# One inference step of a two-layer hybrid backbone: the last head's rows written into the preparation's buffers, six rows prepared in the loop instead of four, attention's bounds and scales computed in the loop, the key weights issued behind a transpose

## The chip, the core and the metric

The kernel runs on one core of one Trainium2 chip. The metric is the device time of one execution in microseconds (us). A core has five engines with a program of their own each: TensorE for matmuls (PE in the profile, PEld its weight loads), VectorE (DVE), ScalarE (ACT), GpSimd (POOL) and SyncE (SP), which here only issues DMA transfers. They meet through semaphores.

## The reference

Two layers, each a modulated RMS norm, a mixer with a SiLU gate, an output projection and a residual. Layer 0 is bidirectional gated linear attention with 4 heads, layer 1 softmax attention with 8 query and 2 key heads on 1024 latent and 256 cached tokens. The 256 prompt tokens run through both layers too. Width is 1024. Cut to what matters:

```python
def step(S, inp):                       # one chunk of the scan, per head and direction
    qi, ki, vi, gi = inp
    b = jnp.cumsum(gi, axis=2)
    ...
    o = jnp.einsum("bhts,bhsv->bhtv", a, vi) + jnp.einsum("bhtk,bhkv->bhtv", qe, S)
    S = jnp.exp(b_last[:, :, 0, :])[..., None] * S + jnp.einsum("bhsk,bhsv->bhkv", ki * jnp.exp(b_last - b), vi)
...
o = rms_norm(o_f + flip(o_b), onorm).reshape(B, T, GLA_VD)
y = (o * jax.nn.silu(gate)) @ w_out     # gla_mixer
xs = xs + gt_s * out_s                  # the residual
...
q = rms_norm(q.reshape(B, T, ATT_HEADS, HEAD_DIM), qn)    # attn_project
k = rms_norm(k.reshape(B, T, ATT_KV_HEADS, HEAD_DIM), kn)
keys = jnp.concatenate([ks_, cache_k[:, i]], axis=1)
vals = jnp.concatenate([vs, cache_v[:, i]], axis=1)
s = jnp.einsum("bqhgd,bkhd->bhgqk", qblk, keys) * scale
```

## The kernel before

The 1280 tokens are 10 rows of 128 (`NT`); rows 0 and 1 are the prompt. Every large product is made of three matmuls with 16-bit halves (high × high, high × low, low × high), so each activation row and each weight is scaled by a power of two and split into two halves `hi` and `lo`; the inverse of a weight's scale is kept in a column `inv`.

**The loop** (`gla`) has 50 slots, one for each head and row, in ten for each of four heads and ten more in which the last head is only finished. In a slot, the values and gates of a row are made (`value_gate`), one direction's scan is advanced (`outer`, `local`) and the other direction of the head before is finished: `combine` (a scan step: POOL makes the state `Sc` from DVE's `Wc`, PE multiplies it, the output tile is called `o`, `U`, `z` or `cs`, DVE adds and makes the next `Wc`) and `gated` (DVE multiplies with the gate's tile `gx`, SP stores the 256 columns of this head into the DRAM tensor `og_d`). Beside that, `filler` and a list of jobs work on what later parts need: the weights of the next head, the split of the attention's weights into DRAM (`split_ahead`), the output weights (`fill_out`, slots 30 to 38), and in the last slots the first output rows. Weights and other pieces are staged through the pool `wst`, which has two buffers of 1 MB; in the last slots one of them holds the residual's gates (`gate_load`).

**A row of layer 0's output** is prepared by `out_load` (a reload of the row, 128x1024, from `og_d`) and `out_prep` (absolute maximum on DVE, a power of two, the high half on ACT, the low half on DVE, two DMA transposes on SP into `hT_hi` and `hT_lo`), and used by `residual` (72 matmuls on PE into the banks `y`, 24 of them 128x512 and 48 of them 128x256, in the loop into the banks `A` and `kt`; scale and add on DVE) and by the modulation for layer 1. Four rows (2 to 5) are prepared in the loop, and two of them (2 and 3) get their residual there.

**`gla_out`** makes the other rows after the loop: per row n the residual, the preparation of row n + 2, the modulation (`mod_tile`, with two transposes) and the keys and values of an earlier row (`key_tile`, 48 matmuls into the bank `kv`, transposes into `kT`). At its start it loads the cache and the key weights `w_kv` (four transfers on SP) and computes what attention needs: `att_setup` the bounds, that is the largest absolute values of the norms' weights and of the cached keys and values, taken over the partitions by matmuls against the identity (`pow2`), and `key_setup` the scales of keys and values.

The order on each engine is set when the program is built: a scheduler simulates the program, and each piece has a priority that the table `LATER` shifts by name. An engine runs its instructions, and SP its transfers, in that fixed order. `issue_after(x)` puts a piece behind the instruction x in the order.

Of the kernel before, what the change touches and what calls it, by code (L numbers as in the profile page):

```python
# [17 lines left out]
P = 128  # L18
D = 1024
# [20 lines left out]
PREP = (42, 43, 45, 46)  # L40
EARLY = (45, 47)
# [31 lines left out]
    "x.prep": -90,  # L73
# [3 lines left out]
    "x.mod": 60,  # L77
# [18 lines left out]
    "gate9": 220,  # L96
    "combine9": -140,
    "jobs9": -150,
    "filler9": 150,
    "x.key8": 150,  # L100
    "eres": 100,
    "emod": -40,
# [4 lines left out]
    "x.key": -30,  # L107
# [17 lines left out]
LN_EXP_SET = 6  # L125


class K:
# [151 lines left out]
    def split_ahead(self, name, j, st):  # L280
# [7 lines left out]
        keep[j] = self.t(self.const, [P, 1], F32, f"inv_{name}{j}")  # L288
# [547 lines left out]
    def gated(self, h, i, og, r, g):  # L836
        nc = self.nc
        nc.vector.scalar_tensor_tensor(g, og, r, g, ALU.mult, ALU.mult)
        nc.sync.dma_start(self.og_d[i, :, h * DV : h * DV + DV], g)
# [17 lines left out]
    def gla_init(self):  # L857
# [4 lines left out]
        self.jobs = []  # L862

# [148 lines left out]
    def gla_out(self, wo, early, n0):  # L1012
# [3 lines left out]
        self.inv_h = self.inv_h1  # L1016
# [14 lines left out]
        for n in range(n0, NT):  # L1031
# [36 lines left out]
            if n == n0:  # L1068
                d, inv = self.ahead["kv"]
                wkv = []  # L1070
                for j, (hi, lo) in enumerate((
                    [t[:, :, 256:512] for t in self.nw[0:2]], (half[:, 0], half[:, 1])
                )):
                    nc.sync.dma_start(hi, d[:, j, 0])
                    nc.sync.dma_start(lo, d[:, j, 1])
                    wkv.append((hi, lo, 256))
                with self.tc.issue_after(last):
                    with self.later("x.setup"):
                        self.att_setup(*ckv)
                    with self.later("x.kset"):  # L1080
                        self.key_setup(*ckv, inv)
# [80 lines left out]
    def att_load(self):  # L1162
# [6 lines left out]
        c = self.t(self.wst, [P, KT, 256], F32, "wst").rearrange("p k n -> p (k n)")  # L1169
        ck, cv = (c[:, 512 * j : 512 * j + 512].rearrange("p (t h d) -> p t h d", t=2, h=2) for j in range(2))  # L1170
        nc.sync.dma_start(ck, I["cache_k"][0, 0].rearrange("(t p) h d -> p t h d", p=P))
        nc.sync.dma_start(cv, I["cache_v"][0, 0].rearrange("(t p) h d -> p t h d", p=P))
        return ck, cv

    def att_setup(self, ck, cv):
        nc, ap = self.nc, self.ap
        m = self.t(self.sm, [P, 4], F32, "amx", bufs=1)
        for j, t in enumerate((self.qn, self.kn)):
            nc.vector.tensor_reduce(m[:, j : j + 1], t, AX.X, ALU.max, apply_absolute_value=True)
        nc.vector.tensor_scalar(m[:, 0:2], m[:, 0:2], 16.0, None, ALU.mult)  # L1180
        for j, t in enumerate((ck, cv)):
            nc.vector.tensor_reduce(
                m[:, 2 + j : 3 + j], t.rearrange("p t h d -> p t (h d)"), AX.XY, ALU.max, apply_absolute_value=True
            )
        nc.vector.tensor_tensor(m[:, 1:2], m[:, 1:2], m[:, 2:3], ALU.max)
        s, inv = self.pow2(m, 4)
        self.asc = self.t(ap, [P, 4], F32, "asc")
        nc.vector.tensor_copy(self.asc, s)
        self.sexp = self.t(ap, [P, 1], F32, "sexp")
# [659 lines left out]
```

## Time and profile before

| | us |
|---|---|
| median of 3 runs | 1254.11 |
| lowest and highest | 1251.12, 1257.43 |
| the profiled execution | 1256.39 |
| its span, first to last instruction | 1254.6 |
| PE busy | 1193.2 |
| DVE busy | 942.8 |
| ACT busy | 689.5 |

The span is read from left to right: the modulation's weights and first rows until about 95 us, the loop's slots until about 548 us, the output rows of layer 0 with keys and values until about 700 us, attention, and layer 1's output. Line numbers (L214) are those of the kernel before. L214 is the helper that issues all three-fold matmuls, so it is read by its tiles (`mm` values, gates and pieces of queries and keys in the loop, `A` and `kt` the two residuals in the loop, `y` the output rows after it, `kv` the key tiles). In a timeline the value in brackets is the engine's idle time ahead of the instruction, and what ended it.

### The profile page before, as it was taken

To read this page: it belongs to the slowest core of one execution; us is meant where nothing else is said; L and a number is where in the kernel's file an instruction comes from. 1 tells how busy PE (TensorE), PEld (TensorE's weight loads), DVE (VectorE), ACT (ScalarE), POOL (GpSimd) and SP (SyncE) were. 2 spreads that over 40 slices of the span, in tenths; PEclk is the share of its full clock that TensorE was granted. 3 is DMA by queue.
4 is the path that set the end of the run, shared out by engine and by line. 5 is a ranking of instruction groups with operands and counts; after the bars stand their busy time and mean duration, and the time that the engine had idled before them with its cause. 6 is when DMAs were issued, how large, how long until landed. Compare 5 with 4: busy or idle time off the path is not lost. (4 is left out here: it accounts for less than half of the span.)

```text
span 1254.6 us, 22383 instructions
## 1 busy us (share of the span) xinstructions
PE 1193.2 (95%) x7990; PEld 781.4 (62%) x7990; DVE 942.8 (75%) x2188; ACT 689.5 (55%) x1698; POOL 326.6 (26%) x566
## 2 busy tenths in 40 slices
PE   4899999999999999898999899999999999989998
PEld 3467765655556557665776666767766657665444
DVE  4787879879788799769875687877766687785653
ACT  2664666647656567623333577666676676663110
POOL 0132123223321243311213434332232342310000
PEclk9999999999999999899999999999999999999999
DMA  9511565456555545589974887767868466978432
GB/s 377 194 65 73 202 210 191 160 176 207 164 180 179 159 124 164 142 237 248 260 191 130 182 157 132 140 132 151 185 135 151 110 123 132 195 139 208 163 135 84
DMA packets 317664, 209.74 MB, mean 167 GB/s; under 512 B 257094, under 2 KB 294254, under 8 KB 309232
## 3 DMA queue, kind: packets, MB, share of 16 engines
q1 hardware_dynamic: 310400, 190.78, 59.1%
q10 hardware_dynamic: 4688, 10.57, 2.4%
q0 software_dynamic: 2464, 6.95, 1.9%
q8 instruction: 63, 1.03, 0.3%
q14 instruction: 49, 0.40, 0.1%
HBM read 107.57 MB, written 39.35 MB: 117 GB/s over the span
## 5 line engine op out<-in xcount | busy, mean ns | idle before, releaser
L214 PEld LDWEIGHTS <-hT_hi 128*128 128x128 f16 x1920 | 187.8, 98 | 120.6 <-DMA hT_hi<-oghl 3.8
L214 PE MATMUL mm<-whi,hT_hi 128*128 128x512 f16 (+1 forms) x576 | 200.2, 348 | 0.5 <-ACT gx L679 0.4
L214 PE MATMUL mm<-whi,hT_lo 128*128 128x512 f16 (+1 forms) x576 | 200.3, 348 | 0.0
L214 PE MATMUL mm<-wlo,hT_hi 128*128 128x512 f16 (+1 forms) x560 | 194.2, 347 | 0.9 <-DVE wlo L276 0.9
L214 PEld LDWEIGHTS <-whi 128*128 128x128 f16 x1232 | 120.2, 98 | 63.8 <-issue 4.4
L1285 PE MATMUL S<-kT,wst 128*128 128x512 f16 (+1 forms) x624 | 140.2, 338 | 7.1 <-ACT p L1293 6.1
L214 PE MATMUL mm<-hT_hi,whi 128*128 128x256 f16 (+1 forms) x480 | 141.0, 294 | 3.7 <-ACT gx L1328 2.4
L1318 DVE SCALAR_TENSOR_TENSOR phl<-p,srec,phl 128x1280 f16<-128x1280 f32 (+1 forms) x80 | 107.0, 1337 | 49.5 <-ACT phl L1317 33.3
L214 PE MATMUL mm<-hT_lo,whi 128*128 128x256 f16 (+1 forms) x480 | 141.0, 294 | 0.0
L214 PE MATMUL mm<-hT_hi,wlo 128*128 128x256 f16 (+1 forms) x480 | 141.0, 294 | 0.0
L214 PEld LDWEIGHTS <-hT_lo 128*128 128x128 f16 x960 | 94.2, 98 | 62.5 <-issue 1.3
L214 PE MATMUL mm<-PT,vh 128*128 128x256 f16 x672 | 117.9, 279 | 9.3 <-DMA PT<-phl 6.3
L1288 DVE TENSOR_REDUCE smx<-S 128x1 f32<-128x1280 f32 (+1 forms) x80 | 101.3, 1271 | 27.0 <-PE S L1285 26.9
L1293 ACT ACTIVATE p<-S,snb,sexp 128x1280 f32<-128x1280 f32 (+1 forms) x80 | 99.1, 1238 | 12.6 <-DVE phl L1318 7.2
L1285 PEld LDWEIGHTS <-wst 128*128 128x128 f16 x624 | 60.9, 98 | 57.3 <-issue 7.1
L214 PE MATMUL mm<-PT,vl 128*128 128x256 f16 x336 | 93.9, 279 | 0.0
L1315 POOL TENSOR_SCALAR phl<-p,srec 128x1280 f16<-128x1280 f32 (+1 forms) x40 | 52.8, 1319 | 107.0 <-DVE srec L1309 62.7
L214 PEld LDWEIGHTS <-vh 128*128 128x128 f16 x672 | 66.7, 100 | 21.1 <-issue 6.0
L214 PEld LDWEIGHTS <-wlo 128*128 128x128 f16 x616 | 60.2, 98 | 29.8
L1124 POOL TENSOR_TENSOR rope<-hx,ropet 128x64 f32<-128x64 f32 x160 | 53.3, 363 | 84.0 <-ACT hx L1249 61.6
L237 DVE TENSOR_REDUCE wmx<-wst 128x1 f32<-128x512 f32 x104 | 65.1, 675 | 3.0 <-DMA wst<-in_att_w 2.0
L205 POOL TENSOR_TENSOR hrs<-hrsa,mhalf 128x2 f32<-128x2 f32 x50 | 39.5, 792 | 81.2 <-DVE hrsa L203 80.7
(383 smaller groups left out, 2682.7 us busy)
## 6 DMA issues: line engine op xcount, KB each, us to landing
wada<-in_w_ada SPq DMA_DIRECT2D x16, 1024.0 KB, 5.4
wst<-in_att_w SPq DMA_DIRECT2D x14, 1024.0 KB, 5.4
wst<-in_gla_w_in SPq DMA_DIRECT2D x12, 1024.0 KB, 5.3
og_d<-gx SPq DMA_DIRECT2D x40, 128.0 KB, 1.9
og_d<-og POOLq DMA_DIRECT2D x40, 128.0 KB, 3.0
wst<-og_d SPq DMA_DIRECT2D x5, 1024.0 KB, 6.1
xr<-x_d SPq DMA_DIRECT2D x9, 512.0 KB, 3.8
out<-xr ACTq DMA_DIRECT2D x17, 256.0 KB, 2.0
```

What stands on the lines that cost most here:

```text
L205: nc.gpsimd.tensor_tensor(r, a, self.mhalf[:, 0:w], ALU.pow)
L214: self.pe = self.nc.tensor.matmul(out, a, b, start=k == 0 and j == 0, stop=k == n - 1 and j == 2).ins
L237: nc.vector.tensor_reduce(mx[:, j : j + 1], st[:, 2 * j : 2 * j + 2, :], AX.XY, ALU.max, apply_absolute_value=True)
L1124: nc.gpsimd.tensor_tensor(tv[:, h, :, w, :], xv[:, h, :, 1 - w, :], sn[:, :, w, :], ALU.mult)
L1285: nc.tensor.matmul(S[:, a : a + n], x, y, start=m == 0, stop=m == 2)
L1288: last = nc.vector.tensor_reduce(mx, S, AX.X, ALU.max).ins
L1293: nc.scalar.activation(p, S, AF.Exp, scale=self.sexp, bias=nb, accum_out=den)
L1315: nc.gpsimd.tensor_scalar(hi, p, r, 2.0 ** 14, ALU.mult, ALU.mult)
L1318: nc.vector.scalar_tensor_tensor(lo, p, r2, hi, ALU.mult, ALU.subtract)
```

## The change

- Rows 2, 3 and 4 of the last head no longer go through `og_d`. In slot 39 (`ROWS`) their buffers are set up, two rows in one buffer of `wst` and one in a buffer of `split`, and the 768 columns of heads 0 to 2 are loaded into them; `gated` writes the last head's 256 columns there, without a store.
- Six rows (2 to 7) are prepared in the loop, in slots 40, 41, 42, 45, 46 and 48, instead of four in 42, 43, 45 and 46. The two residuals in the loop stand in slots 43 and 46 instead of 45 and 47.
- The bounds are a job of slot 11, with loads of the cache and of the norms' weights of their own (four transfers on SP); the cache is loaded again for its use. The scales are a job of slot 42: five small DVE instructions on a table `inv_a` of all the weights' inverse scales, in place of columns that were multiplied one by one.
- The loads of `w_kv` stand behind the last transpose of the rows prepared in the loop.
- The table `LATER` has other numbers for eight names, and one name less.

The diff, with the parts left out that only rename columns:

```diff
-PREP = (42, 43, 45, 46)
-EARLY = (45, 47)
+ROWS = 39
+PREP = (40, 41, 42, 45, 46, 48)
+EARLY = (43, 46)
...
-    "x.prep": -90,
+    "x.prep": -150,
...
-    "combine9": -140,
-    "jobs9": -150,
-    "filler9": 150,
+    "combine9": 70,
+    "jobs9": 220,
+    "filler9": 15,
...
+BOUNDS, SCALES = 11, 42
...
     def gated(self, h, i, og, r, g):
         nc = self.nc
+        a = slice(h * DV, h * DV + DV)
+        if h == GH - 1 and i in self.direct:
+            nc.vector.scalar_tensor_tensor(self.direct[i][:, a], og, r, g, ALU.mult, ALU.mult)
+            return
         nc.vector.scalar_tensor_tensor(g, og, r, g, ALU.mult, ALU.mult)
-        nc.sync.dma_start(self.og_d[i, :, h * DV : h * DV + DV], g)
+        nc.sync.dma_start(self.og_d[i, :, a], g)
...
-                    nc.sync.dma_start(hi, d[:, j, 0])
-                    nc.sync.dma_start(lo, d[:, j, 1])
+                    with self.tc.issue_after(self.tr):
+                        nc.sync.dma_start(hi, d[:, j, 0])
+                        nc.sync.dma_start(lo, d[:, j, 1])
...
+    def bounds_load(self):
+        t = self.t(self.wst, [P, KT, 256], F32, "wst").rearrange("p k n -> p (k n)")
+        self.cache(t)
+        for j, n in enumerate(("att_qnorm", "att_knorm")):
+            self.nc.sync.dma_start(t[:, D + HD * j : D + HD * j + HD], self.I[n].to_broadcast([P, HD]))
+        return self.bounds, t
+
+    def bounds(self, t):
+        nc = self.nc
+        m = self.t(self.small, [P, 4], F32, "wmx")
+        nc.vector.tensor_reduce(
+            m[:, 2:4], t[:, 0:D].rearrange("p (j n) -> p j n", j=2), AX.X, ALU.max, apply_absolute_value=True
+        )
+        nc.vector.tensor_reduce(
+            m[:, 0:2], t[:, D : D + 2 * HD].rearrange("p (j n) -> p j n", j=2), AX.X, ALU.max,
+            apply_absolute_value=True,
+        )
         nc.vector.tensor_scalar(m[:, 0:2], m[:, 0:2], 16.0, None, ALU.mult)
...
         s, inv = self.pow2(m, 4)
...
+            if slot == BOUNDS:
+                k.jobs.append(k.bounds_load())
+            if slot == SCALES:
+                k.jobs.append((k.scales,))
...
+            if slot == ROWS:
+                t = k.t(k.wst, [P, KT, 256], F32, "wst").rearrange("p k n -> p (k n)")
+                u = k.t(k.spl, [P, 2, KT // 2, 256], F16, "split").rearrange("p j k n -> p (j k n)").bitcast(F32)
+                for n, a in enumerate((t[:, 0:D], t[:, D:], u)):
+                    k.direct[NTP + n] = a
+                for n in (1, 0, 2):
+                    load(k.direct[NTP + n][:, 0 : D - DV], k.og_d[NTP + n, :, 0 : D - DV])
             if slot in PREP:
                 n = PREP.index(slot)
-                a = k.t(k.wst, [P, KT, 256], F32, "wst").rearrange("p k n -> p (k n)")[:, 0:D]
                 b = [k.t(k.qkp, [P, 512], F32, f"{j}{n % 2}").bitcast(F16) for j in "qk"]
-                to = k.out_load(NTP + n, a, b)
+                if NTP + n in k.direct:
+                    to = NTP + n, k.direct[NTP + n], b
+                else:
+                    a = k.t(k.wst, [P, KT, 256], F32, "wst").rearrange("p k n -> p (k n)")[:, 0:D]
+                    to = k.out_load(NTP + n, a, b)
```

Three places of the programs. The first is PE in the last slots of the loop, the steps of the last head's scan (`o`, `U`, `z`, `cs` from `Sc`). Before:

```order
L214 MATMUL mm_6748<-whi_1555_5986,hT_lo_74 128x256
L826 MATMUL o_6680<-Sc_6676,qe_6278 128x256
L826 MATMUL U_6731<-Sc_6727,qe_6141 128x256
L826 MATMUL z_6786<-Sc_6782,qe_6010 128x256
L826 MATMUL cs_6855<-Sc_6851,qe_5893 128x256
L826 MATMUL o_6920<-Sc_6916,qe_5759 128x256
L214 LDWEIGHTS hT_hi_73
```

Five steps stand in a row. After, three stand in a row:

```order
L219 MATMUL mm_6797<-whi_1552_6003,hT_lo_74 128x256
L832 MATMUL o_6703<-Sc_6699,qe_6295 128x256
L832 MATMUL U_6769<-Sc_6765,qe_6158 128x256
L832 MATMUL z_6835<-Sc_6831,qe_6027 128x256
L219 LDWEIGHTS hT_hi_73
```

Then 24 matmuls of a value or gate tile follow, and behind them the next two steps (`cs`, `o`) and 24 more.

The second place is DVE at the same scan, around the fifth `Wc`; `wm` from a row's buffer (`wst` or `split`) is the maximum of a row's preparation. Before:

```order
L795 TENSOR_TENSOR Wc_6918<-Sc_6916,u_1550_5975 128x256
L828 TENSOR_TENSOR og_6922<-o_6920,oa_1554_5984 128x256
L203 TENSOR_SCALAR orsa_6862<-ossq_6860 128x1
L795 TENSOR_TENSOR Wc_7056<-Sc_7054,u_1518_5862 128x256
L203 TENSOR_SCALAR orsa_6927<-ossq_6925 128x1
L783 COPY Wc_7285<-u_1431_5571 128x256
L320 SCALAR_TENSOR_TENSOR ls_6720<-gx_6718,ls_6720 128x256
L1001 TENSOR_REDUCE wm_1783_6799<-wst_6744 128x1
```

After, from the row behind the fourth `Wc`:

```order
L208 TENSOR_SCALAR orsa_6842<-ossq_6840 128x1
L188 TENSOR_SCALAR p2e_6719<-p2c_6717 128x1
L846 SCALAR_TENSOR_TENSOR wst_6581<-og_6705,ors_6712,gx_6622 128x256
L334 TENSOR_TENSOR gx_6756<-gx_6756,ls_6758 128x256
L190 TENSOR_SCALAR p2s_6721<-p2e_6719 128x1
L846 SCALAR_TENSOR_TENSOR split_6582<-og_6771,ors_6778,gx_6690 128x256
L192 TENSOR_SCALAR p2i_6723<-p2e_6719 128x1
L834 TENSOR_TENSOR og_6991<-cs_6989,oa_1593_6136 128x256
L1015 TENSOR_REDUCE wm_1777_6781<-wst_6581 128x1
L801 TENSOR_TENSOR Wc_7054<-Sc_7052,u_1547_5992 128x256
L848 SCALAR_TENSOR_TENSOR gx_6756<-og_6837,ors_6844,gx_6756 128x256
L1015 TENSOR_REDUCE wm_1796_6854<-split_6582 128x1
```

Before, the first row's maximum stands behind the sixth `Wc`. Now the gates are written into the rows' buffers, and the maximum of row 3 stands ahead of the fifth `Wc`, that of row 4 behind it; that of row 2 (not shown) stands ahead of the third.

The third place is SP at the start of the output rows: the loads of the cache, of the key weights `w_kv`, and the transposes of the prepared rows. Before:

```order
L1172 DMA wst_7372<-in_cache_v 128x2x256
L1008 DMA_TRANSPOSE hT_lo_74<-k_1846_7103 128x8x128
L488 DMA_TRANSPOSE hT_hi_73<-split_7019 128x8x128
L488 DMA_TRANSPOSE hT_lo_74<-split_7019 128x8x128
L995 DMA og_7357<-og_d_64 128x1024 x2
L1024 DMA xr_7471<-in_x_sample 128x1024
L1074 DMA whi_1555_5986<-w_kv_1478 128x8x256
L1075 DMA wlo_1556_5987<-w_kv_1478 128x8x256
L839 DMA og_d_64<-gx_7276 128x256
L1074 DMA wkv_7358<-w_kv_1478 128x2048
L1075 DMA wkv_7358<-w_kv_1478 128x2048
```

After:

```order
L1021 DMA_TRANSPOSE hT_hi_73<-q_1882_7349 128x8x128
L849 DMA og_d_64<-gx_7329 128x256
L1187 DMA wst_7423<-in_cache_k 128x2x256
L1188 DMA wst_7423<-in_cache_v 128x2x256
L1022 DMA_TRANSPOSE hT_lo_74<-k_1883_7350 128x8x128
L1088 DMA whi_1552_6003<-w_kv_1481 128x8x256
L1089 DMA wlo_1553_6004<-w_kv_1481 128x8x256
L1009 DMA og_7412<-og_d_64 128x1024
L1037 DMA xr_7508<-in_x_sample 128x1024
L1088 DMA wkv_7413<-w_kv_1481 128x2048
L1089 DMA wkv_7413<-w_kv_1481 128x2048
```

The last gated row's store, which stood between the key weights, now stands ahead of them, and so does the second transpose of row 7 (`k`). The transposes of the early modulation (`split`) stand ahead of the first of these rows.

More of the change, by code (lines that the diff above doesn't have):

```diff
@@ L106 @@
     "wo3": 245,
-    "x.key": -30,
+    "x.key": -150,
     "s.v": 150,
@@ L1347, in load_w @@
         w = self.wload(name, place, later)
[L1348 removed]
+        return w, w[2]
     def query_start(self):
```

81 lines of the change are left out of this document (37 added, 44 removed).

## The prediction, made before the changed kernel ran

> **What bounds the kernel now.** I read the page first: busy time and share of each engine, then the chain of waits that ended last.
>
> ```profile
> PE 1193.2 (95%) x7990; PEld 781.4 (62%) x7990; DVE 942.8 (75%) x2188; ACT 689.5 (55%) x1698; POOL 326.6 (26%) x566
> PE 30%; DMA 4%; DVE 3%; ACT 1%; issue 1%; POOL 0%; ACTq 0%; POOLq 0%; SPq 0%
> ```
>
> TensorE (PE) is busy in 1193.2 of 1254.6 us, so all that waits can give back in the whole program is 61 us. The change takes no matmul away from PE. So the next view is the busy time by windows (window, its length, then busy us of PE, its weight loads, DVE, ACT, POOL; the granted clock; the DMA share) around the places that the change works in: the end of the loop, the first output rows, and what follows.
>
> ```profile
> 498.50:548.10 49.60, 43.97 (x304) 31.74 (x304) 37.76 (x103) 25.45 (x67) 14.28 (x21) 0.93 0.54 146
> 548.10:610.00 61.90, 55.93 (x418) 40.26 (x417) 50.78 (x133) 21.61 (x43) 7.54 (x12) 1.00 1.10 269
> 610.00:700.00 90.00, 90.00 (x667) 65.06 (x665) 62.95 (x141) 32.04 (x89) 27.55 (x60) 1.00 0.76 183
> ```
>
> PE idles 49.60 − 43.97 = 5.6 us in the loop's end, 61.90 − 55.93 = 6.0 us in the first rows, and not at all in the 90 us after: what is won ahead of 610 passes through those 90 us unchanged. In the first row the clock is 0.93, the only dip of the three. The view of PE's waits (engine, line, waited for: us, times, longest) names the causes:
>
> ```profile
> PE y L214 <- DMA hT_hi<-oghl: 3.5, 1, 3.5
> PE kv L172 <- DVE p2e L183: 1.8, 1, 1.8
> PE cs L826 <- POOL Sc L791: 1.6, 1, 1.6
> PE U L826 <- POOL Sc L791: 1.4, 1, 1.4
> PE z L826 <- POOL Sc L791: 0.9, 1, 0.9
> PE y L214 <- DMA hT_lo<-oghl: 0.7, 1, 0.7
> PE o L826 <- POOL Sc L791: 0.6, 1, 0.6
> ```
>
> **Term 1, the output rows.** PE's timeline (start, us, instruction, idle before it and its releaser) places three of them in the output rows:
>
> ```profile
> 548.15 0.38 PE L214 MATMUL y<-whi,hT_hi 128*128 128x512 f16 x1
> ...
> 568.88 0.27 PE L214 MATMUL y<-wada,hT_lo 128*128 128x256 f16 x1
> 570.96 0.23 PE L172 MATMUL kv<-ident,amx 128*128 128x128 bf16 x1 [1.81 <-DVE p2e L183]
> ...
> 579.67 0.39 PE L214 MATMUL y<-whi,hT_hi 128*128 128x512 f16 x1 [3.50 <-DMA hT_hi<-oghl]
> ...
> 593.87 0.39 PE L214 MATMUL y<-whi,hT_lo 128*128 128x512 f16 x1 [0.66 <-DMA hT_lo<-oghl]
> ```
>
> They sum to 5.97, all of the idle time of this window. The first is the bounds' transpose on PE, which stands in PE's order ahead of the first key tile. With the bounds in slot 11 it is not there: −1.81. The other two are rows 6 and 7, whose preparation started only in this phase, and which are now prepared in the loop. When are they ready there? A row needs its store, reload, reduce, two halves and two transposes. Before, four rows do this one behind the other, since one staging buffer is free for the reload:
>
> ```profile
> 523.80 1.22 DVE L1001 TENSOR_REDUCE wm<-wst 128x1 f32<-128x1024 f32 x1 [1.94 <-DMA wst<-og_d]
> ...
> 533.26 1.22 DVE L1001 TENSOR_REDUCE wm<-wst 128x1 f32<-128x1024 f32 x1 [2.04 <-DMA wst<-og_d]
> ...
> 542.45 1.22 DVE L1001 TENSOR_REDUCE wm<-wst 128x1 f32<-128x1024 f32 x1 [2.31 <-DMA wst<-og_d]
> ```
>
> ```profile
> 545.45 1.23 SPq L1007 DMA_TRANSPOSE hT_hi<-q  x1
> ...
> 548.67 1.86 SPq L1008 DMA_TRANSPOSE hT_lo<-k  x1
> ```
>
> A turn is 9.5 us, and the second transpose is issued 6 us behind the reduce (548.67 − 542.45). Rows 2 to 4 now skip store and reload, so only rows 5, 6 and 7 take such turns, in the buffer that rows 2 and 3 leave. The page has the reload (KB, median us to landing):
>
> ```profile
> wst<-og_d SPq DMA_DIRECT2D x5, 1024.0 KB, 6.1
> ```
>
> If the halves of row 3 are out of the buffer near 520 (row 2's came at 518 before, and its reload is gone), row 5's reduce stands near 527, those of rows 6 and 7 near 536 and 546; they are transposed by 542 and 552 and, with an allowance of 7 us for landing, ready by 549 and 559. PE takes 20.8 us for two rows (548.15 to 568.88), so it wants row 6 at about 567 and row 7 behind a key tile at about 583. Some 20 us are in hand: −3.50 − 0.66.
>
> The key weights could be late in their place. Before, they leave SP here:
>
> ```profile
> 557.27 0.38 SPq L1074 DMA_DIRECT2D whi<-w_kv  x1
> ...
> 558.44 4.45 SPq L839 DMA_DIRECT2D og_d<-gx  x1
> 562.92 0.43 SPq L1074 DMA_DIRECT2D wkv<-w_kv  x1
> ```
>
> The second pair stood 4.45 us behind the last gated row's store and was still in time. After, all four stand behind that store and behind row 7's second transpose, so they go at about 553 to 557, and PE reads them from about 568, since the first key tile now stands between the matmuls of row 6. With 6 to 7 us for landing they are there some 4 us ahead. Nothing is added; if row 7 slips by more than that, each further us costs one. Term 1 is **−6.0**; its bounds are −6.0, and −2.5 if the key weights inherit a wait of 3.50.
>
> **Term 2, the scan in the loop's end.** The last head's o steps wait for POOL's Sc, this for DVE's Wc, this for the Sc before:
>
> ```profile
> 503.13 0.70 PE L826 MATMUL U<-Sc,qe 128*128 128x256 f32 x2 [1.36 <-POOL Sc L791]
> 504.68 0.70 PE L826 MATMUL z<-Sc,qe 128*128 128x256 f32 x2 [0.85 <-POOL Sc L791]
> 507.03 1.22 PE L826 MATMUL cs<-Sc,qe 128*128 128x256 f32 x2 [1.65 <-POOL Sc L791]
> 508.88 1.22 PE L826 MATMUL o<-Sc,qe 128*128 128x256 f32 x2 [0.63 <-POOL Sc L791]
> ```
>
> ```profile
> 507.00:509.00 2.00, 1.34 (x3) 0.63 (x3) 1.99 (x7) 0.95 (x4) 1.82 (x3) 0.50 0.19 66
> 509.00:511.00 2.00, 2.00 (x8) 1.32 (x9) 1.10 (x4) 1.15 (x6) 1.50 (x3) 0.50 0.81 195
> 511.00:513.00 2.00, 2.00 (x11) 1.44 (x10) 0.78 (x3) 1.97 (x8) 1.49 (x3) 0.50 0.52 207
> ```
>
> From 507 to 513 PE is busy for 5.3 us at half clock, which is 2.7 us of work: 2.7 more are lost, and no view of waits shows them. The stretch of 49.6 us is thus 5.6 of waits, 2.7 of clock and 41.3 of work. Before, five o steps stand in a row on PE. After, 24 matmuls of 128x256 stand between the third and the fourth (some 2.6 us, at a quarter of the 10.4 us that a row of 24 wide and 48 such matmuls takes) and cover about one step of the chain (1.55, 2.35 and 1.85 us between the starts above). Against that, DVE, which runs the chain and is already full ahead of it, gets the reduces of rows 2, 3 and 4 between its Wc's, each of 1.22:
>
> ```profile
> 475.00:500.00 25.00, 24.07 (x177) 18.83 (x176) 24.51 (x75) 19.83 (x52) 7.47 (x12) 1.00 0.47 148
> ```
>
> I laid DVE's new order over these durations, Wc, Sc, o in turn. Row 2's reduce stands ahead of the third Wc, row 3's ahead of the fifth, row 4's behind it. PE's waits come out as 1.2 in the first three steps, 1.4 and 2.1 at the fourth and fifth, 1.6 for row 2's transposes: 6.3, an estimate. At full clock the stretch takes 41.3 + 6.3 = 47.6, that is −2.0; with the half clock again, 50.3, +0.7; with every wait and the clock won, −8.3. I take **−2.0**, because the low stretch (PE busy 1.34 of 2 us and less) is now broken by dense matmuls.
>
> [...]
>
> **Term 3, the loop at slot 11.** The bounds bring four loads through one staging buffer on SP, ahead of head 2's query and key weights, and on DVE a reduce of 1024 elements (1.22), a short one and some ten small instructions: about 3.5 us. The 16 small instructions that go lay at 564 to 590, where they cost nothing by themselves. Around the place:
>
> ```profile
> 200.00:225.00 25.00, 24.51 (x164) 15.71 (x162) 22.96 (x63) 15.19 (x46) 10.97 (x19) 1.00 0.63 225
> ```
>
> ```profile
> 199.51 0.64 SPq L843 DMA_DIRECT2D wst<-in_gla_w_in  x1
> ...
> 202.95 0.33 SPq L229 DMA_DIRECT2D wst<-in_att_w  x1
> ```
>
> ```profile
> 220.21 0.27 PE L214 MATMUL mm<-hT_hi,whi 128*128 128x256 f16 x1 [0.49 <-ACT gx L679]
> ```
>
> ```profile
> 220.51 2.27 DVE L276 SCALAR_TENSOR_TENSOR wlo<-wst,p2s,whi 128x512 f16<-128x512 f32 x3
> ```
>
> The load of 199.51 takes the turn of 202.95, 3.4 us later, so the fill that ends at 222.78 ends near 226. PE started on that piece at 220.21, beside the fill; about 2 us of other matmuls now go ahead of it. A stall between 0 and 3.4 remains; 3.4 − 2 = 1.4 is left if PE was right behind the fill, less where it was not, and I take **+0.5**. A gain is excluded here: nothing is removed. The remaining edits I cost at nothing: the five scale instructions of slot 42 (0.14 to 0.22 each, counted with the chain's DVE time), the second load of the cache, 0.5 MB on queues that carry 0.54 of their share at 498 to 548, and the table in place of copies.
>
> **Sum.** −6.0 − 2.0 + 0.5 = −7.5. The profiled execution took 1256.39, so its like would take 1248.9; it lies 2.3 above the median of the runs shown, 1254.11, which gives **1246.6**.
>
> **Rivals.** *The scan eats it* (0.25): the three reduces add 1.22 each to PE's waits and the half clock comes again: +3.6 in place of −2.0, so −1.9 in all, 1252. For it: DVE at 24.51 of 25. Against: the 24 matmuls between the steps. *All is won* (0.12): −6.0 − 8.3, 1240. For it: 37.76 of 49.60 us busy on DVE leave room on average; against: the chain's own steps of about 2 us. *The queue falls behind* (0.13), the slower side: SP issues in order, and per output row with its key tile there are six transposes and three loads or stores. PE takes 10.4 + 5.2 = 15.6 us for such a row; transposes at 1.2 to 2.7 us take 7 to 16. The lead of the four rows still prepared in this phase, counted in PE's order, shrinks from about 23 us to 15.6. From the point where SP needs over 15.6 us a row, each of the four waits as row 6 did, 3.50: +14.0, in all +6.5, 1261. For it: the DMA share of 1.10 from 548 to 610. Against: the same load per row at 610 to 700 with PE at 90.00 of 90.00. *The 1.81 is hidden anyway* (within the first): PE would then wait longer for row 6; but 36 and more matmuls stand between the two waits and both are idle time, so they add.
>
> **How the numbers follow.** The forecast has 0.50. A measurement of this kernel can tell some 0.5%, 6.3 us, from no change, so faster means below 1247.8. Three quarters of the forecast (whose own range is 1242 to 1250) lie there, with the large gain: 0.50. Within the bound are its rest and the first rival: 0.35. Slower is the queue's case with the upper end of term 3: 0.15. The range is 1239 (all won) to 1256 (the first rival with 3.4 in term 3).
>
> **What would show it.** Right: no wait of a kv matmul for p2e, none of y for hT from 548 to 610; PE at its whole time from the first y on; the first y near 546; the clock above 0.97 in the loop's end. Wrong: a kv wait for the key weights, a y wait for a transpose, an o wait for Sc above 2.5, a wait for wlo near 220 to 226, or new waits behind 700, where PE's order is the same and the gain should arrive whole.

## The result, and the profile after

| | before | changed |
|---|---|---|
| median of 7 runs, us | 1255.56 | 1249.33 |
| lowest and highest | 1251.12, 1258.47 | 1246.71, 1250.21 |
| the profiled execution | 1256.39 | 1248.91 |
| its span | 1254.6 | 1247.1 |

The changed kernel takes 0.9947 of the time before (95% interval 0.9929 to 0.9966). That is 0.5%, about what can be told from no change. The profiled execution came out at 1248.91, where the sum of the prediction had 1248.9. The total does not show that the sum was right, as its parts below do not agree with it.

The page's busy times, of the changed kernel, are nearly those of before: the same 7990 matmuls, 0.7 us less on PE, 16 small DVE instructions fewer.

```profile
PE 1192.5 (96%) x7990; PEld 780.1 (63%) x7990; DVE 941.4 (75%) x2172; ACT 690.0 (55%) x1698; POOL 324.3 (26%) x566
```

The busy time by windows, of the changed kernel, over the same stretches as before (columns as in the prediction):

```profile
498.50:548.10 49.60, 44.49 (x312) 32.31 (x310) 43.60 (x123) 30.74 (x75) 13.83 (x20) 0.97 0.59 149
548.10:610.00 61.90, 59.95 (x450) 43.83 (x448) 42.94 (x90) 20.13 (x46) 10.92 (x18) 1.00 1.06 253
```

In the output rows PE idles 61.90 − 59.95 = 1.95 us where it idled 6.0. In the loop's end it idles 5.1 where it idled 5.6, and DVE is busy 43.60 of 49.60 where it had 37.76. The view of PE's waits of the changed kernel no longer has a `kv` wait for `p2e` or a `y` wait for `hT`. It has others:

```profile
PE y L219 <- DVE whi L996: 2.0, 1, 2.0
PE o L832 <- POOL Sc L797: 1.9, 1, 1.9
...
PE o L832 <- DVE asc L1211: 1.2, 1, 1.2
```

PE's timeline of the changed kernel has them in place, in the last slots of the loop and in the first output row:

```profile
502.01 0.27 PE L219 MATMUL mm<-whi,hT_hi 128*128 128x256 f16 x1 [0.60 <-ACT gx L685]
...
505.47 0.70 PE L832 MATMUL U<-Sc,qe 128*128 128x256 f32 x2 [0.24 <-POOL Sc L797]
507.26 0.70 PE L832 MATMUL z<-Sc,qe 128*128 128x256 f32 x2 [1.09 <-POOL Sc L797]
...
511.93 0.70 PE L832 MATMUL cs<-Sc,qe 128*128 128x256 f32 x2 [1.31 <-POOL Sc L797]
514.49 1.22 PE L832 MATMUL o<-Sc,qe 128*128 128x256 f32 x2 [1.86 <-POOL Sc L797]
...
549.20 0.38 PE L219 MATMUL y<-whi,hT_hi 128*128 128x512 f16 x1
...
556.50 0.27 PE L219 MATMUL y<-whi,hT_hi 128*128 128x256 f16 x1 [1.95 <-DVE whi L996]
```

The first `y` starts at 549.20, later than before (548.15). To see where the 7.5 us between the spans come from, cut each execution at five points of PE's timeline: a matmul ahead of slot 11's pieces (192.91 before, 192.03 changed), one some 107 us behind it (299.79 and 301.71), the first `y` of the output rows, the end of the last key tile, the end of the last score matmul `S`. Between the first two points PE has the same matmuls in both kernels, and four more in the changed one, those of the bounds. Both kernels were profiled a second time among the experiments. Each column is the time from the point before:

| us | to the first point | slot 11 and behind | to the first `y` | to the last key tile | to the last score | rest | span |
|---|---|---|---|---|---|---|---|
| before | 192.9 | 106.9 | 248.4 | 142.2 | 436.1 | 128.1 | 1254.6 |
| before, again | 191.6 | 107.0 | 248.5 | 143.4 | 436.0 | 128.2 | 1254.6 |
| changed | 192.0 | 109.7 | 247.5 | 137.6 | 432.0 | 128.3 | 1247.1 |
| changed, again | 191.4 | 109.9 | 246.3 | 140.6 | 431.6 | 126.4 | 1246.2 |
| difference of the means | −0.5 | +2.9 | −1.5 | −3.7 | −4.2 | −0.8 | −7.9 |
| predicted | 0 | +0.5 | −2.0 | −6.0 | 0 | 0 | −7.5 |

The programs are the same up to the first point, so its −0.5 is not of the change. Slot 11 cost more than forecast, the rest of the loop won nearly what was forecast, the output rows won less, and about half of the gain arose in attention, in which PE's order is the same in both programs.

**What the rows' new wait is.** The `y` matmul of 556.50 waits for a bank that row 3's early residual still holds. Its last step on DVE reads the bank (`kt`, line 996). DVE's timeline of the changed kernel:

```profile
550.27 1.22 DVE L1015 TENSOR_REDUCE wm<-wst 128x1 f32<-128x1024 f32 x1 [1.01 <-DMA wst<-og_d]
551.41 0.68 DVE L996 TENSOR_TENSOR whi<-A,whi 128x512 f32<-128x512 f32 x1
...
554.43 1.28 DVE L1019 SCALAR_TENSOR_TENSOR k<-wst,p2s,q 128x1024 f16<-128x1024 f32 x1
...
555.76 0.69 DVE L996 TENSOR_TENSOR whi<-kt,whi 128x512 f32<-128x512 f32 x1
```

Row 7's maximum (550.27) stands in the middle of that residual, and its low half (554.43) right ahead of the last step. The maximum itself waited 1.01 us for row 7's reload. The residual's last step starts behind both, at 555.76, and PE's matmul behind that. The reload had not been late for the transposes. It was late for what stands behind it on DVE.

**Where attention's gain is.** Two stretches of 20 us of attention run partly at half clock before, in both profiles, and at full clock after, in both. By windows, before:

```profile
970.00:990.00 20.00, 17.86 (x135) 13.84 (x133) 10.47 (x35) 11.50 (x41) 7.07 (x15) 0.91 0.61 135
1100.00:1120.00 20.00, 16.93 (x115) 11.84 (x114) 15.63 (x23) 10.99 (x19) 3.81 (x4) 0.91 0.78 146
```

The same places in the changed kernel, whose pieces come 3.5 and 6.7 us earlier:

```profile
964.00:984.00 20.00, 17.96 (x143) 13.80 (x142) 11.93 (x37) 12.75 (x42) 7.08 (x15) 1.00 0.68 127
1093.00:1113.00 20.00, 15.87 (x118) 11.27 (x117) 17.22 (x24) 11.84 (x20) 3.76 (x4) 1.00 0.79 145
```

In the first place, 143 matmuls are done with nearly the same busy time, instead of 135. Over the second half of attention, from 900.00 to 1126.90 before and from 896.40 to 1119.20 after:

```profile
900.00:1126.90 226.90, 216.72 (x1541) 152.01 (x1541) 167.93 (x349) 153.93 (x395) 72.01 (x123) 0.98 0.70 139
```

```profile
896.40:1119.20 222.80, 213.29 (x1540) 150.34 (x1541) 168.22 (x349) 154.16 (x395) 72.86 (x123) 1.00 0.70 142
```

The same 1540 matmuls take 216.72 − 213.29 = 3.4 us less busy time, while idle time falls only from 10.2 to 9.5; in the second profiles the busy times are 217.15 and 213.36. So in this half it is clock, not waits. The first half takes 209.6 us in the first profile of each, though the changed kernel has a half-clock stretch of its own there (0.83 from 730 to 740 in both profiles). The wait inside the second stretch is even longer where the clock stays up, before:

```profile
1106.21 0.39 PE L214 MATMUL mm<-PT,vh 128*128 128x256 f16 x2 [2.24 <-DMA PT<-phl]
```

and changed:

```profile
1099.49 0.39 PE L219 MATMUL mm<-PT,vh 128*128 128x256 f16 x2 [2.61 <-DMA PT<-phl]
```

Around these two waits, in stretches of 3.41 us, before:

```profile
1103.65:1107.07 3.42, 1.18 (x11) 0.82 (x10) 3.42 (x4) 2.12 (x4) 0.00 (x0) 1.00 0.81 192
1107.07:1110.48 3.41, 3.41 (x18) 2.45 (x17) 3.15 (x4) 1.12 (x3) 0.41 (x1) 0.50 0.76 142
```

and changed:

```profile
1094.55:1097.96 3.41, 1.78 (x9) 0.78 (x8) 3.41 (x5) 0.80 (x3) 0.91 (x2) 1.00 1.19 184
1097.96:1101.37 3.41, 1.88 (x18) 1.69 (x19) 3.41 (x5) 2.95 (x4) 0.00 (x0) 1.00 0.84 155
```

Before, PE was busy for 1.18 of the 3.42 us that hold the wait of 2.24 us, and the 3.41 us behind them have half clock. In the changed kernel the wait of 2.61 us lies across the two stretches shown, in which PE was busy for 1.78 and 1.88 us; the clock is 1.00 in both and in the 3.41 us behind them. What keeps it up there, these two cases do not show.

### The profile page after: what moved, and what is told of

It is laid out like the page before. It is cut to its first block, busy times and chain, and to the rows that moved or that the text cites. A ratio compares the mean times of both kernels' runs of the same rounds, so it can differ in the third digit from the quotient of the medians.

```text
span 1247.1 us, 22361 instructions
## 1 busy us (share of the span) xinstructions
PE 1192.5 (96%) x7990; PEld 780.1 (63%) x7990; DVE 941.4 (75%) x2172; ACT 690.0 (55%) x1698; POOL 324.3 (26%) x566
## 5 line engine op out<-in xcount | busy, mean ns | idle before, releaser
L1343 DVE SCALAR_TENSOR_TENSOR phl<-p,srec,phl 128x1280 f16<-128x1280 f32 (+1 forms) x80 | 107.0, 1337 | 48.4 <-ACT phl L1342 33.8
L219 PE MATMUL mm<-PT,vh 128*128 128x256 f16 x672 | 114.9, 275 | 8.9 <-DMA PT<-phl 5.1
L1318 ACT ACTIVATE p<-S,snb,acol 128x1280 f32<-128x1280 f32 (+1 forms) x80 | 99.1, 1238 | 13.4 <-DVE phl L1343 7.7
```

Of the source, the lines that this page charges most:

```text
L219: self.pe = self.nc.tensor.matmul(out, a, b, start=k == 0 and j == 0, stop=k == n - 1 and j == 2).ins
L1318: nc.scalar.activation(p, S, AF.Exp, scale=self.sexp, bias=nb, accum_out=den)
L1343: nc.vector.scalar_tensor_tensor(lo, p, r2, hi, ALU.mult, ALU.subtract)
```

## The experiments

Ratios are to the kernel before, timed beside it on the same chip, with 95% intervals; times are medians; diffs are against the changed kernel unless said otherwise.

**Three parts taken back one at a time, and one part alone.** The first is the kernel before with only the bounds moved to slot 11 and the scales to slot 42 (diff against the kernel before, beside the new functions; `LATER`, `PREP` and `EARLY` stay old):

```diff
+ROWS = None
 PREP = (42, 43, 45, 46)
 EARLY = (45, 47)
+BOUNDS, SCALES = 11, 42
```

> The kernel before with one part of the change: bounds in slot 11, scales in slot 42. Theory (terms stand by themselves): the kv wait of 1.81 for p2e is gone and the loop near slot 11 pays about 1.1 us of new PE idle time between 205 and 222 us; row 6 still makes PE wait, 2.5 to 3.5 us. PE idle time in the first output rows 3.2 to 4.2 instead of 6.0. Time against before: -1 us (-3 to +1). Rival (the 1.81 was hidden anyway): the wait for hT of row 6 grows to about 5.3, idle time in these rows stays 6.0, time against before +1.

1262.95 us, 1.0062 (1.0043 to 1.0082): slower. PE's timeline from 548 to 610 has one long wait:

```profile
582.01 0.61 PE L220 MATMUL y<-whi,hT_hi 128*128 128x512 f16 x1 [9.91 <-DMA hT_hi<-oghl]
```

That is the 3.50 of before plus the bounds' 1.81, and some 4.6 more. Without the bounds' transpose the scheduler put the first key tile (5.2 us) behind row 6 instead of ahead of it, so this cover was gone too. The transpose was late on SP, behind the key weights and the modulation's transposes:

```profile
562.46 3.43 SPq L1088 DMA_DIRECT2D wkv<-w_kv  x1
...
567.50 3.17 SPq L495 DMA_TRANSPOSE hT_hi<-split  x1
570.77 5.23 SPq L495 DMA_TRANSPOSE hT_lo<-split  x1
576.09 3.81 SPq L1022 DMA_TRANSPOSE hT_hi<-oghl  x1
```

The rival "the 1.81 is hidden anyway" holds for the bounds alone, and more than that is lost. At slot 11 this kernel takes 111.4 us between the first two points of the table, 4.5 more than before, where 1.1 was expected.

The second is the changed kernel with bounds and scales where they were:

```diff
-            if slot == BOUNDS:
-                k.jobs.append(k.bounds_load())
-            if slot == SCALES:
-                k.jobs.append((k.scales,))
```

> The changed kernel with the bounds and the scales back behind the loop. Theory: the loop near slot 11 is as before (no PE wait over 0.6 between 200 and 225), and a kv or y wait of 1 to 2 us appears in the output rows. Time against before -5.5 us (-7.5 to -3), that is about +0.7 against the changed kernel. Rival (the moved bounds carry the gain, also in attention): against before -2 or less of a gain.

1257.37 us, 1.0019 (0.9995 to 1.0044), not told apart from the kernel before; 5.5 us below it was expected. The first `y` came at 547.5, 1.7 ahead of the changed kernel's first profile but level with its second (547.6). PE's timeline has the bounds' wait again, and then waits for the key weights:

```profile
568.88 0.29 PE L177 MATMUL kv<-ident,wmx 128*128 128x128 bf16 x1 [2.92 <-DVE nt_ra L208]
576.07 0.27 PE L219 MATMUL kv<-whi,hT_hi 128*128 128x256 f16 x1 [0.52 <-DMA whi<-w_kv]
578.84 0.37 PE L219 MATMUL kv<-wlo,hT_hi 128*128 128x256 f16 x1 [2.28 <-DMA wlo<-w_kv]
```

The third sends all six rows through `og_d`, as the four went before:

```diff
-ROWS = 39
+ROWS = None
```

> The changed kernel with rows 2 to 4 of the last head again stored to DRAM and reloaded; six rows are still prepared in the loop. Theory (the direct rows are what lets six rows be ready in time): six reload turns of 9.5 us push row 7's transposes 10 to 25 us later than 557, PE waits for hT or for the key weights by 3 to 15 us between 550 and 620; time against before from -3 to +9. Rival (the direct rows mostly burden the scan): the reduces leave the chain, PE's idle time in 498 to 549 falls below 4, and the time is as the changed kernel's or 1 to 2 us better.

1263.08 us, 1.0059 (1.0039 to 1.008). Row 7's second transpose goes at 578.20, and the key weights, held behind it, follow and are late; a `y` matmul waits 3.22 besides. SP and then PE:

```profile
578.20 1.23 SPq L1022 DMA_TRANSPOSE hT_lo<-k  x1
579.47 0.59 SPq L1088 DMA_DIRECT2D whi<-w_kv  x1
```

```profile
584.52 0.37 PE L219 MATMUL kv<-whi,hT_hi 128*128 128x256 f16 x1 [7.85 <-DMA whi<-w_kv]
```

The fourth does not hold the key weights behind the transpose:

```diff
-                    with self.tc.issue_after(self.tr):
-                        nc.sync.dma_start(hi, d[:, j, 0])
-                        nc.sync.dma_start(lo, d[:, j, 1])
+                    nc.sync.dma_start(hi, d[:, j, 0])
+                    nc.sync.dma_start(lo, d[:, j, 1])
```

> The changed kernel with the key weights not held behind the last transposes. Theory (they have slack either way): no kv wait in either, the first key tile starts as in the changed kernel; time against the changed kernel within 1 us, against before -6.5 (-8.5 to -4.5). Rival (their 2 MB delay the reload and the transposes of row 7 when they go earlier): a y wait for hT of 1 to 4 us between 550 and 600, time against before -5 to -2.

1250.57 us, 0.9966 (0.9942 to 0.999), not told apart from the changed kernel. The `y` wait is 2.95 here, and no `kv` matmul waits. Within what these intervals can tell, some 3 us, where the key weights stand is of no account as long as the rest is as it is.

**The waits that were new.** Four kernels try to take away what the changed kernel's profile showed: the wait for `asc` at slot 11, the residual behind row 7's maximum, the maxima in the scan. The bounds in another slot:

```diff
-BOUNDS, SCALES = 11, 42
+BOUNDS, SCALES = 33, 42
```

> The changed kernel with the bounds in slot 33 instead of 11, where DVE is busy 18.96 of 25 us and no other load waits for the staging buffers. Theory (slot 11 pays because DVE and the staging buffers are full there): PE's waits of 1.16, 0.24 and 0.16 near 207 to 222 fall to 0.5 in all, no new wait near 400 to 425, the first y starts 1 us earlier, time 1 us below the changed kernel's. Rival (the bounds cost about 1 us of PE wherever they are, since o waits for their DVE work): the same wait appears near 400 to 425, time as the changed kernel's.

1270.29 us, 1.0127 (1.0091 to 1.0164), the slowest of all. At slot 11 a wait of 0.95 for `gx` is left, and the stretch between the first two points of the table falls to 107.4 us, as in the run without the bounds' move. But between 480 and 520 there are waits of `kt` matmuls (0.23, 1.31), for `gx` (0.85, 1.81, 1.54) and for `Sc` (2.51, 1.68, 0.24, 1.55); the first `y` came at 558.5. That a staging buffer taken at slot 33 makes the output weights late is a reading of the order only; no run here shows it.

Row 7's preparation behind row 3's residual (`early_res` is the residual's last instruction):

```diff
+                def job(*a):
+                    if a[0] == NTP + 5:
+                        with tc.issue_after(k.early_res):
+                            prep.append(k.placed("eprep", k.out_prep, *a))
...
-                k.jobs.append((lambda *a: prep.append(k.placed("eprep", k.out_prep, *a)), *to))
+                k.jobs.append((job, *to))
```

> The changed kernel with row 7's preparation ordered behind the residual of row 3. Theory (the 1.95 wait of y for DVE is the residual of row 3 held up behind row 7's maximum, which itself waits for its reload): the y wait is below 0.4, row 7 and the key weights come about 2 us later and are still in time, PE idle time from the first y to 687 falls from 1.95 to below 0.5, time 1.5 to 2 us below the changed kernel's. Rival (the key weights have no slack, or the wait moves to the next row): a kv wait for w_kv or a y wait for hT of 1 to 3 us takes its place, time as the changed kernel's or above.

1254.61 us, 1.0004 (0.9984 to 1.0024). The `y` wait fell from 1.95 to 0.17, so its cause is shown. The gain was given back, and more: row 3's modulation transposes now stand ahead of the key weights on SP, and PE waits for these. SP, then PE:

```profile
563.09 3.08 SPq L494 DMA_TRANSPOSE hT_hi<-split  x1
566.34 1.23 SPq L494 DMA_TRANSPOSE hT_lo<-split  x1
...
568.72 1.59 SPq L1088 DMA_DIRECT2D whi<-w_kv  x1
```

```profile
575.31 0.37 PE L219 MATMUL kv<-whi,hT_hi 128*128 128x256 f16 x1 [4.56 <-DMA whi<-w_kv]
577.08 0.37 PE L219 MATMUL kv<-wlo,hT_hi 128*128 128x256 f16 x1 [0.97 <-DMA wlo<-w_kv]
```

The maxima of rows 2 to 4 taken over 64 columns and multiplied by 64, which leaves most of the three reduces out:

```diff
-        nc.vector.tensor_reduce(mx, og, AX.X, ALU.max, apply_absolute_value=True)
+        if i in self.direct:
+            nc.vector.tensor_reduce(mx, og[:, 0:64], AX.X, ALU.max, apply_absolute_value=True)
+            nc.vector.tensor_scalar(mx, mx, 64.0, None, ALU.mult)
+        else:
+            nc.vector.tensor_reduce(mx, og, AX.X, ALU.max, apply_absolute_value=True)
```

> The changed kernel in which the maxima of rows 2 to 4 are taken over 64 of 1024 columns and multiplied by 64: this leaves out most of three maxima, 3.4 us of DVE time inside the scan. Theory (these maxima eat what the 24 matmuls between the steps cover): PE's waits for Sc from 502 to 516 fall from 4.5 to between 1 and 2.5 us, the clock stays at 1.00, the first y starts 3 to 5 us earlier, time 3 us (2 to 5) below the changed kernel's. Rival (the chain of Wc, Sc and o sets the pace, not the maxima): waits for Sc stay above 3.5, time within 1 us of the changed kernel's.

1258.01 us, 1.0032 (1.0012 to 1.0053): slower, not 3 us faster. The scan's waits for `Sc` fell from 4.5 (0.24 + 1.09 + 1.31 + 1.86) to 2.8 (0.24 + 1.75 + 0.79):

```profile
506.59 0.70 PE L832 MATMUL U<-Sc,qe 128*128 128x256 f32 x2 [0.24 <-POOL Sc L797]
509.03 0.84 PE L832 MATMUL z<-Sc,qe 128*128 128x256 f32 x2 [1.75 <-POOL Sc L797]
...
513.86 0.60 PE L832 MATMUL cs<-Sc,qe 128*128 128x256 f32 x2
515.24 0.70 PE L832 MATMUL o<-Sc,qe 128*128 128x256 f32 x2 [0.79 <-POOL Sc L797]
```

That is not what the reduces cost. In this profile the granted clock is 0.68 from 508 to 512 and 0.89 from 512 to 516. The 24 matmuls ahead of `cs` took 4.4 us (509.66 to 514.02), where the changed kernel's took 2.8 (507.84 to 510.62), and `cs` has no wait. The run with row 7 behind has all three maxima, a clock of 0.57 from 508 to 512, and waits of 2.98. From the start of `U` to that of the last `o` it is 8.65 us here, and 9.02 and 8.87 in the two profiles of the changed kernel, so the reduces cost the chain 0.2 to 0.4 us. The first `y` came at 548.4, between those two profiles (549.2 and 547.6). Behind it the scheduler made another order: the second pair of key weights leaves SP only at 580.93, and four `kv` waits sum to 7.2 (1.16 + 1.31 + 3.45 + 1.26). The time of the whole says nothing on the reduces.

Both moves, slot 33 and row 7, together:

> The changed kernel with both, the bounds in slot 33 and row 7's preparation behind the residual of row 3. Theory (terms add): 2.5 to 3 us below the changed kernel's, about 1246 to 1247, 0.7% below before. Rival (one move takes the other's gain, as parts of the change did): less than 1 us below the changed kernel's.

1268.88 us, 1.0117 (1.0088 to 1.0147), where 0.7% below before was expected: the loss of slot 33 again, with a first `y` at 559.1.

**Row 7 behind, and the key weights ahead.** If the loss of the row 7 move is the key weights' place on SP, loading them behind row 6's last transpose should give it back:

```diff
-        self.tr = nc.sync.dma_start_transpose(to[1], lo).ins
+        self.tr6, self.tr = self.tr, nc.sync.dma_start_transpose(to[1], lo).ins
...
-                    with self.tc.issue_after(self.tr):
+                    with self.tc.issue_after(self.tr6):
```

> The kernel of the run on row 7 (its preparation behind the residual of row 3), with the key weights held behind row 6's transposes instead of row 7's, so that the first pair leaves SP ahead of row 7's transposes and of row 3's modulation. Theory (in that run the gain of 1.95 was lost only because the key weights went behind the two transposes of row 3's modulation, issued at 568.7 and read at 570.7): no kv wait for the first pair, y wait below 0.4, PE idle time in the output rows 0.2 to 1.5, time 1 to 2 us below the changed kernel's. Rival (the transfers of 548 to 600 saturate their engines, so whatever goes first makes another late): a wait of 2 to 5 us for the second pair of key weights, for xr or for hT takes its place; time 1 us or more above the changed kernel's.

1251.76 us, 0.9972 (0.9958 to 0.9986): 2.9 us less than without this edit, but not below the changed kernel. The first pair is in time; the second pair still goes behind the modulation's transposes (571.90 and 572.38), and PE waits 1.23 and 2.02 us for it, as the rival had it.

The changed kernel itself ran beside it, unedited:

> The changed kernel once more, unchanged, to compare with the others on one chip and to see what one profile varies. Theory: the stages from 64 us to the first y and from there to the last key tile agree with the first profile within 1 us, attention (last key tile to last score) lies within 432 to 436, since only that stage varied among kernels with one order there; time 0.4 to 0.7% below before. Rival (attention's 4 us belong to the change): attention is at 432 to 433 again, and the kernel before would always be near 436.

1250.36 us, 0.9959 (0.9943 to 0.9975). Its profile has the `y` wait at 3.27, the waits for `Sc` at 4.4 in sum, and full clock in the scan; a dip stands at 556 to 560 instead, where the granted clock is 0.64 behind the longer `y` wait. The output rows take 3.0 us more than in the first profile, where 1 was expected. In the two places of attention the clock is 1.00 again (964 to 984 and 1093 to 1113).

Then the second pair was moved up as well, by a priority for these loads and with the table of rotations behind them:

```diff
+    "x.wkv": -600,
...
+                    with self.tc.issue_after(self.tr6), self.later("x.wkv"):
...
-                with self.tc.issue_after(self.tr):
+                with self.tc.issue_after(kvl):
                     nc.sync.dma_start(self.ropet, self.I["k_rope"])
```

> The kernel of the run before last but with a higher place of the key weights in SP's order: the first pair both ahead of row 2's modulation, the second pair straight behind the transposes of row 3's modulation, ahead of the loads of xr and of the reloaded row; k_rope behind them. Theory (in that run the second pair was issued at 571.9 and 572.4 and made PE wait 3.25 in all; each us earlier on SP is a us less of wait): the second pair leaves 1.5 to 2 us earlier, the kv waits fall from 3.25 to between 0.5 and 2, no other wait takes their place, time 1 to 2 us below that run's, equal to the changed kernel's or up to 1 us below. Rival (saturated transfers: the sum of what 548 to 600 must move sets the end): xr or the reloaded row come later and PE or DVE wait for them by as much; time as that run's.

1247.77 us, 0.9952 (0.9936 to 0.9967). The `y` wait is 0.26 and one `kv` wait of 0.87 is left; a wait of 1.54 for `vl` on DVE is new at 593.96. Against the changed kernel's ratio it is not told apart, so there is no version here that clearly beats it.

The kernel before, unedited, beside it:

> The kernel before once more, unchanged. Theory (attention varies by itself): attention from the last key tile to the last score lies somewhere in 432 to 438, not always near 436; the waits of 1.8, 3.5 and 0.7 in the output rows and the half clock near 506 to 513 are there again, stage from the first y to the last key tile 142 within 1 us. Rival (the change makes attention faster): attention at 436 again, with the same half-clock places.

1255.65 us, 1.0008 (0.9993 to 1.0022): the measurement tells no change as no change. The waits of the output rows were 2.27, 1.71 and 1.45, which sum to 5.4 instead of 6.0. Half clock stands in attention at the same places as in the first profile, 0.91 from 970 to 990 and from 1100 to 1120, and once more, 0.91 from 710 to 720 and 0.75 from 720 to 730. So far the rival came true.

## Why the prediction came out, and which of its steps failed

**The total.** 1246.6 was forecast and 1249.33 measured, within the forecast's own range of 1242 to 1250. That is 6.2 us less than before instead of 7.5. Two errors of the sum, some 2 us each, and a term that it did not have cancelled out. That is luck.

**Term 1, right in kind and too large.** All three waits went, as forecast: the bounds' 1.81 and rows 6 and 7. The window idles 4.0 us less in one profile, and over two profiles of each the stage is 3.7 shorter, not 6.0. The step that failed is "Nothing is added". It followed the key weights and the transposes, but not what row 7's preparation stands in front of on DVE: row 3's residual, and behind that the bank that PE wants. The wait is 1.95 in one profile and 3.27 in the other, and 0.17 when row 7 is put behind the residual. The estimate for row 7 itself was 4 us off: its maximum stood at 550.27, not 546, since its turn began later.

The slack of the key weights, "some 4 us ahead", came out by two errors that cancelled. It used 6 to 7 us for landing, and the view of DMA issues between 545 and 600 has, for the changed kernel:

```profile
whi<-w_kv SPq DMA_DIRECT2D x1, 512.0 KB, 10.4
```

against 7.5 before. The load left SP at 559.35, so it landed near 569.8; but PE reads it first at 573.88, not at 568. No `kv` matmul waits. In the runs in which something else came ahead of these loads on SP, PE waited for them (4.56 us with row 7 behind, 7.85 without the direct rows).

**Term 2, near in size, not for the reason given.** The rest of the loop is 0.9 us shorter in one profile and 2.1 in the other, where 2.0 was forecast. The scan's waits were estimated at 6.3, and came to 4.5 for `Sc` and 0.6 for `gx`, 5.1. That the three maxima make these waits is not borne out, since the run with short maxima shortens the chain by only 0.2 to 0.4 us. From `U` to the last `o` the chain takes 9.02 us where it took 5.75 before; what else lengthens it stays open. And "because the low stretch is now broken by dense matmuls" held in one profile only. In the other PE is busy for 0.70 of 3.41 us at the fourth step, and half clock follows in the next 3.41 us:

```profile
510.87:514.28 3.41, 0.70 (x2) 0.30 (x2) 3.41 (x17) 1.74 (x5) 3.15 (x4) 1.00 0.59 137
514.28:517.69 3.41, 3.20 (x13) 2.21 (x14) 3.41 (x7) 3.38 (x10) 1.32 (x3) 0.50 0.91 222
```

No wait in this scan is over 1.86 us, where the estimate had up to 2.1, and half clock came all the same. In the second profile the waits for `Sc` sum to 4.4, nearly as much, and the clock is 1.00 from 507 to 519. What sets the two profiles apart is not shown.

**Term 3, too small.** The stall was put between 0 and 3.4 and taken at 0.5. Over the same matmuls the changed kernel takes 2.8 us more than before. Before, changed, and the changed kernel without the bounds' move:

```profile
192.91:299.79 106.88, 106.39 (x631) 62.57 (x629) 89.64 (x241) 66.22 (x177) 32.61 (x57) 1.00 0.54 179
```

```profile
192.03:301.71 109.68, 108.12 (x635) 62.53 (x633) 93.01 (x252) 66.56 (x176) 30.75 (x56) 1.00 0.55 180
```

```profile
192.40:299.97 107.57, 106.45 (x631) 62.58 (x629) 89.47 (x241) 66.15 (x176) 33.11 (x57) 1.00 0.55 178
```

So the bounds cost 2.1 us here, and 0.7 came without them. Of the 2.8, 1.1 is idle time and 1.7 is busy time, which a reading of waits alone does not see; why four small matmuls more should make 1.7 the rows do not show. The longest wait and the DVE instruction that the view names for it:

```profile
220.30 0.67 PE L832 MATMUL o<-Sc,qe 128*128 128x256 f32 x2 [1.16 <-DVE asc L1211]
```

```profile
220.08 0.15 DVE L1211 COPY asc<-p2s 128x4 f32<-128x4 f32 x1
```

The place was right (slot 11, 220), but PE did not wait for the fill's halves. Whether it waited for the bounds' copy `asc` is not shown: `og`, which empties the bank `o` that this step writes, ended on DVE right ahead of it (219.75 to 220.16), behind two of the fill's maxima.

**What was not in the sum: attention.** "New waits behind 700, where PE's order is the same and the gain should arrive whole" allowed only for a loss. The order is the same, and no new waits came, but the stage is 4.2 us shorter. In its second half it is shown that this is clock: 3.4 us of busy time for the same matmuls, half clock at two places in both profiles of before and in neither of the changed kernel. The waits there are not shorter.

The dips do not follow the length of the wait: one of 2.24 us before is followed by half clock, one of 2.61 after is not, as shown above. In the two profiles of before the dips lie alike (0.91 from 970 to 990 and from 1100 to 1120 in both). Over all fourteen profiles of this study the stage took between 431.6 and 437.8 us, 433.0 with the bounds alone and 437.8 with the short maxima, so the 4.2 us cannot be counted on as a gain of this change. No run shifted attention by a chosen time with all else unchanged.

**The rivals.** "The scan eats it" had the half clock right for one profile and the sum wrong: the rest of the loop did not lose 3.6 us but won 1.5. "All is won" failed in term 2. "The queue falls behind" did not happen in the changed kernel. Its mechanism is real a little further on: the runs without direct rows, without the bounds' move, and with row 7 behind all ended with key weights late on SP, with 2.8 (0.52 + 2.28) to 9.2 us (7.85 + 1.38) of `kv` waits, a large part of what separates their 1254.6 to 1263.1 from the changed kernel. "The 1.81 is hidden anyway" was dismissed because both waits "are idle time, so they add". With the bounds alone they did not add, since the order changed with the edit.

## What to carry to other kernels

Measure a change of several parts as a whole and part by part: the bounds alone cost 8 us, without the bounds' move nothing was won that can be told from no change, without the direct rows 7 us were lost, and with both 5 to 6 us were won. Where a scheduler sets the order, an edit is also a new order. Read what now stands ahead of each load on its queue and behind each new instruction on its engine, and not only the slack of the piece that was moved. When a total comes out as forecast, cut both traces at the same matmuls of the program before believing the reasons: sums of waits missed most of the cost of slot 11.

## What was not expected of the hardware

- Half clock came without a long wait and stayed away after one. In the scan of the changed kernel no wait is over 1.86 us, but PE is busy 0.70 of the 3.41 us from 510.87, and the next 3.41 us have 0.50. Before, the wait of 3.50 us ahead of 579.67 left PE busy for 0.49 of the 4.00 us from 576, and the clock is 1.00 there and from 580 to 588.
- One and the same kernel had its half clock at the same places in two profiles (before: 0.91 from 970 to 990 and from 1100 to 1120 in both), or at different places (changed: 0.86 from 507 to 519 in one profile; 1.00 there and 0.64 from 556 to 560 in the other). In the second half of attention, with unchanged order, the same 1540 matmuls took 3.4 us more of PE's busy time at a mean clock of 0.98 than at 1.00.
- From 548 to 610, where the DMA share is 1.06, the issue of a transpose into `hT` holds SP's queue between 1.23 us and 7.29 us (below), and a load of the key weights (`whi`, 512 KB) lands 10.4 us behind its issue; before it was 7.5, with the short maxima 13.9. SP's timeline of the changed kernel:

```profile
559.35 0.96 SPq L1088 DMA_DIRECT2D whi<-w_kv  x1
...
570.29 7.29 SPq L494 DMA_TRANSPOSE hT_hi<-split  x1
```
